# Up products by Strassen's seven block products in the feed-forward part of a decoder layer

## The chip, the cores and the metric

The kernel runs on one core of a Trainium2 chip. The metric is the device time of one execution in microseconds. In the profile PE is TensorE (its weight loads are PEld), DVE is VectorE, ACT is ScalarE, POOL is GpSimd, and SP is the engine whose queue issues most loads. The kernel is written with a layer that places semaphores and chooses the order of instructions on each engine when it is built; the order on the chip is then fixed.

## The reference, cut to what matters

The reference is one layer of a decoder: attention, an RWKV time mixing, a gated output projection, and a feed-forward part with a short convolution. It serves 2048 tokens of a prompt and 8 groups of 8 sample tokens, 2112 columns in all. The change lies in the second half:

```
x += (sigmoid(gA) * (A @ w_pa) + sigmoid(gB) * (B @ w_pb)) @ w_o
h = rmsnorm(x) * norm2_g
ug, uv = split(h @ w_up)                 # w_up: 1024 x (2 * 2816)
c = conv_b + sum_j conv_w[j] * ug shifted by 2 - j
x += (gelu(c) * uv) @ w_down
y = rmsnorm(x) * final_g
```

All values are float32. A product is made in three passes: each operand is split into a high part of fewer bits and the rest (hi and lo), and hi x hi, hi x lo and lo x hi are added.

## The kernel before

Everything is stored transposed: 128 features are the partitions of a tile, tokens are its columns. Phase 1 makes the projections, the attention and the time mixing, and leaves the gates and the outputs in DRAM. Phase 2 (`group2`) walks three groups of 704 columns, each in two chunks of 352. In a group:

1. For each of 8 output tiles the products with w_pa and w_pb (one weight tile, `w_ab`), multiplied with the gates, added on POOL and split into hi and lo (`mix`).
2. For each of 8 tiles the product with w_o over both chunks, added to x (`x2`), scaled with norm2_g and split (`h2`), squared and summed over the tiles in `rs`.
3. The second norm's factor is computed from `rs` by small matmuls and some ten short VectorE operations (`rstd_steps`). It isn't applied to `h2`: it multiplies the results. The products of the up tiles can start before it is known; line 1395 applies it to the gate half, and POOL at line 1417 applies it for the value half.
4. 22 gate tiles (`up`) and 22 value tiles (`gate`) in parts of 4, 6, 6 and 6. A tile is a product over 8 blocks of 128 features, three passes and two chunks: 48 matmuls. `up` goes on with the convolution (two taps at line 1405), the GELU by tanh, and `gate` multiplies and splits the result.
5. After each part the product with w_down for 8 tiles, added to `x2`. After the last part the final norm, which runs beside the next group's first products.

Weights come through `weights`: one load of 512 KB on SP's queue into one of two raw buffers, then in two halves a cast on ScalarE to hi (line 354, two buffers) and a subtraction to lo (line 392, three buffers). The subtraction alternates between VectorE and POOL:

```
eng = self.nc.gpsimd if self.wn % self.pool_every == 0 and not self.nopool else self.nc.vector
```

All matmuls are issued at line 287. While `self.ordered` is set, as it is from phase 1 to the end, they keep the order in which the program writes them; all else is put in order by the layer's own planner. Products go to eight PSUM buffers (`acc`).

## Time and profile before

| | us |
|---|---|
| median of 3 runs | 3466.67 (3464.66 to 3475.59) |
| the profiled execution | 3464.11 |
| its span, first to last instruction | 3462.3 |
| TensorE busy | 3288.2 |
| VectorE busy | 2165.3 |
| POOL busy | 1356.5 |
| ScalarE busy | 1313.2 |

Phase 2 begins at some 1529 us and takes the rest of the span. "Busy" is the time in which at least one instruction of the engine was at work. Two matmuls overlap in the records, so the mean duration of one is about twice the distance between two; the distance is read from the starts.

### The profile page before, as it was taken

Reading aid. Unit: us, or ns where it says so; the run is one execution under the profiler, and the core shown is the slowest. Engines: PE = TensorE matmul, PEld = TensorE weight load, DVE = VectorE, ACT = ScalarE, POOL = GpSimd, SP = SyncE. Lnnn points to the kernel's source line nnn. Section 1 sums busy time; section 2 is a strip of 40 time slices with the busy share of each in tenths; the row PEclk is TensorE's granted clock in tenths of the full one; section 3 lists DMA queues with packets and bytes.
Section 4 is the critical chain, followed back from the end, with each engine's and each line's share of the span. In section 5 each row is a group of like instructions: output and inputs, shape, how many; then the busy total and the mean of one; then the engine's idle time right before and its main releaser. Section 6 shows DMA issues by size and latency. Waiting matters only on the chain.

```text
span 3462.3 us, 59729 instructions
## 1 busy us (share of the span) xinstructions
PE 3288.2 (95%) x23574; PEld 3128.4 (90%) x23574; DVE 2165.3 (63%) x3813; ACT 1313.2 (38%) x2658; POOL 1356.5 (39%) x1375
## 2 busy tenths in 40 slices
PE   6889899899899899989999999999999999999998
PEld 6778788788788788879999999999999999999998
DVE  6767758867868858754554545555554654564554
ACT  4444434544545544423332323232232423332332
POOL 4435434435435435233333333533333442343342
PEclk9999989999999999999999999999999999999999
DMA  4442523433433433343122223612222352222222
GB/s 133 153 140 91 154 87 95 136 104 92 142 105 92 141 106 92 116 174 110 58 77 68 66 75 99 203 62 74 62 74 67 93 178 81 68 65 77 61 74 73
DMA packets 165968, 347.51 MB, mean 100 GB/s; under 512 B 59263, under 2 KB 91655, under 8 KB 165687
## 3 DMA queue, kind: packets, MB, share of 16 engines
q1 hardware_dynamic: 138263, 283.60, 26.8%
q0 software_dynamic: 8704, 37.78, 3.3%
q10 hardware_dynamic: 18720, 22.31, 1.8%
q8 instruction: 185, 3.03, 0.4%
q14 instruction: 96, 0.79, 0.1%
HBM read 302.06 MB, written 41.56 MB: 99 GB/s over the span
## 4 chain that ended last, share of the span: by engine, by line
PE 59%; DVE 3%; issue 1%; ACT 1%; DMA 0%; POOL 0%; DVEq 0%; ACTq 0%; POOLq 0%
PE acc L287 57%; PE ps L287 1%; DVE wlo L392 0%; DMA th<-outs 0%; PE psA L287 0%; DVE TX L1000 0%; PE psY L287 0%; ACT whi L354 0%; DVE LN L1002 0%; DVE x L1324 0%; PE ps L290 0%; ACT at L746 0%; DVE XV L1133 0%; DVE t_kk L930 0%; DVE G L972 0%
## 5 line engine op out<-in xcount | busy, mean ns | idle before, releaser
L392 POOL TENSOR_TENSOR wlo<-w,whi 128x512 fp32r<-128x512 f32 (+2 forms) x488 | 700.5, 1436 | 1237.0 <-ACT whi L354 987.8
L287 PE MATMUL acc<-A,whi 128*128 128x352 f32 x4992 | 1007.9, 323 | 2.3 <-DVE A L1288 1.5
L354 ACT CAST whi<-w 128x512 fp32r<-128x512 f32 (+2 forms) x984 | 537.3, 591 | 1228.1 <-PE acc L287 727.1
L287 PE MATMUL acc<-h,whi 128*128 128x384 f32 (+2 forms) x3456 | 914.5, 344 | 19.7 <-ACT raw L664 12.1
L287 PEld LDWEIGHTS acc<-A,whi 128*128 128x128 f32 x4992 | 836.0, 188 | 4.3 <-DVE A L1288 2.5
L287 PEld LDWEIGHTS acc<-h,whi 128*128 128x128 f32 x3456 | 631.6, 197 | 52.5 <-ACT raw L664 16.3
L287 PE MATMUL acc<-h,wlo 128*128 128x384 f32 (+2 forms) x1728 | 588.6, 341 | 22.0 <-DVE wlo L392 21.9
L287 PE MATMUL acc<-A,wlo 128*128 128x352 f32 x2496 | 604.5, 323 | 0.0
L287 PE MATMUL acc<-B,whi 128*128 128x352 f32 x2880 | 582.1, 323 | 0.5 <-DVE B L1291 0.4
L392 DVE TENSOR_TENSOR wlo<-w,whi 128x512 fp32r<-128x512 f32 (+2 forms) x496 | 437.4, 883 | 128.6 <-ACT whi L354 127.2
L287 PEld LDWEIGHTS acc<-B,whi 128*128 128x128 f32 x2880 | 482.3, 188 | 1.1 <-DVE B L1291 1.1
L287 PEld LDWEIGHTS acc<-A,wlo 128*128 128x128 f32 x2496 | 434.3, 188 | 0.1
L287 PEld LDWEIGHTS acc<-h,wlo 128*128 128x128 f32 x1728 | 340.5, 197 | 40.1 <-DVE wlo L392 26.9
L287 PE MATMUL acc<-B,wlo 128*128 128x352 f32 x1440 | 350.2, 323 | 0.0
L1446 DVE TENSOR_TENSOR x<-x,acc 128x352 f32<-128x352 f32 x188 | 89.5, 518 | 304.5 <-PE acc L287 304.5
L287 PEld LDWEIGHTS acc<-B,wlo 128*128 128x128 f32 x1440 | 250.9, 188 | 0.0
L1417 POOL TENSOR_TENSOR ss<-ss,ssq 128x704 f32<-128x704 f32 x66 | 113.0, 1713 | 288.6 <-DVE ss L1416 268.4
L1405 DVE SCALAR_TENSOR_TENSOR cc<-ub,vt,cc 128x704 f32<-128x704 f32 (+1 forms) x132 | 159.4, 1208 | 27.3 <-ACT cc L1399 25.8
L1395 DVE TENSOR_TENSOR ub<-acc,ssq 128x352 f32<-128x352 f32 (+1 forms) x132 | 61.6, 508 | 180.4 <-PE acc L287 179.1
L1413 ACT ACTIVATE ss<-cc 128x704 f32<-128x704 f32 x66 | 52.3, 792 | 174.9 <-DVE cc L1405 116.7
L1291 DVE SCALAR_TENSOR_TENSOR B<-ss,B 128x704 fp32r<-128x704 f32 x66 | 113.5, 1720 | 3.7 <-ACT B L1290 3.7
L1414 DVE SCALAR_TENSOR_TENSOR ss<-ss,cc 128x704 f32<-128x704 f32 x66 | 58.9, 892 | 59.6 <-ACT ss L1413 59.6
(302 smaller groups left out, 3694.5 us busy)
## 6 DMA issues: line engine op xcount, KB each, us to landing
w<-w_in SPq DMA_DIRECT2D x216, 512.0 KB, 3.6
w<-w_ug SPq DMA_DIRECT2D x66, 512.0 KB, 3.5
w<-w_uv SPq DMA_DIRECT2D x66, 512.0 KB, 3.5
w<-w_down SPq DMA_DIRECT2D x72, 384.0 KB, 3.1
th<-gates POOLq DMA_DIRECT2D x48, 352.0 KB, 4.2
gates<-raw ACTq DMA_DIRECT2D x64, 192.0 KB, 2.0
w<-w_ab SPq DMA_DIRECT2D x24, 512.0 KB, 3.9
w<-w_o SPq DMA_DIRECT2D x24, 512.0 KB, 3.5
```

Source lines behind the costliest of these rows:

```text
L287: self.pe(self.nc.tensor.matmul(out, lhsT, rhs, start=start, stop=stop), max(n * (1 if rhs.dtype == F32R else 4) / 2.4, 25))
L354: nc.scalar.copy(out=hi[:, a:b], in_=w[:, a:b])
L392: i = eng.tensor_tensor(**kw)
L1291: nc.vector.scalar_tensor_tensor(out=lo[:, :T], in0=src[:, :T], scalar=scale, in1=hi[:, :T].bitcast(F32), op0=MUL, op1=SUB)
L1395: nc.vector.tensor_tensor(out=ub[:, 2 + a:2 + e], in0=pp[:, :e - a], in1=rs[:, a:e], op=MUL)
L1405: nc.vector.scalar_tensor_tensor(out=cc[:, :n], in0=ub[:, j:j + n], scalar=self.v(wn, f), in1=cc[:, :n], op0=MUL, op1=ADD)
L1413: nc.scalar.activation(out=s[:, :T], in_=cc[:, :T], func=AF.Square, scale=GELU_A)
L1414: nc.vector.scalar_tensor_tensor(out=s[:, :T], in0=s[:, :T], scalar=1.0, in1=cc[:, :T], op0=ADD, op1=MUL)
L1417: nc.gpsimd.tensor_tensor(out=s[:, :T], in0=s[:, :T], in1=rs[:, :T], op=MUL)
L1446: nc.vector.tensor_tensor(out=x2[m][:, a:b], in0=x2[m][:, a:b], in1=pp[:, :b - a], op=ADD)
```

## The change

Two up tiles that lie side by side (features f and f+1), the two halves of their 8 feature blocks, and the two chunks of columns make a 2 x 2 by 2 x 2 product of blocks. The kernel before makes its eight block products. The change makes seven, after Strassen in Winograd's form, and adds them up on VectorE (`product`, `put`). Each block product has 4 feature blocks, three passes and one chunk: 12 matmuls of 352 columns. Four of the seven take a sum of blocks of x (`t1` to `t4`), four a sum of weight blocks (`s1` to `s4`), and the others take the blocks as they are. With sums of both chunks the second norm's factor must be on the operands, so x is multiplied with it before the products: the first chunk while the second one's w_o products run, the second after the last w_o product, in three stages. For this w_o is now walked chunk by chunk. In the first part of a group the first two products of three runs, which need the first chunk alone, are placed ahead of the others, with the order of matmuls fixed there.

The sums of weights are made once, in group 0, by POOL, and written to DRAM (`weight_sums`); later block loads read them there. Two block products share one load buffer, so a weight buffer holds 24 matmuls' worth. All subtractions of weight splits go to VectorE in phase 2 (`nopool`). The factor of one half moves from the splits to the additions after w_o and w_down.

```diff
-            self.bufs = dict(A=16, B=16, x2=8, th=4, tm=2, ub=2, cc=2, ss=2, ssq=1, carry=2, nrm=3)
+            self.bufs = dict(A=56, B=12, x2=8, th=4, ub=2, cc=2, ss=4, u=3, u3=1, ug=1, ssq=1, carry=2, nrm=3)
...
+            self.ordered = False
+            self.sums_d = [[self.dram.tile([128, 4, 4, 128], F32, name=f"sums{x}{i}") for i in range(cfg.ff // 2)] for x in "gv"]
...
+    def gemm2(self, hi, lo, xs, cs=(0, 1), wk0=0):
+
+        outs = [self.pt("acc") for _ in cs]
+        n, w = len(xs), self.cfg.tmax2 // 2
+        for k in range(n):
+            ops = [xs[k](c) for c in cs]
+            for i in range(3):
+                for o, (xh, xl) in zip(outs, ops):
+                    self.mm(o[:, :w], (hi, hi, lo)[i][:, wk0 + k, :], (xh, xl, xh)[i], k == 0 and i == 0, k == n - 1 and i == 2)
...
+    def weight_sums(self, x, i):
...
+        ap = self.A["w_ug" if x == 0 else "w_uv"]
+        v = [self.t("th", [128, self.cfg.tmax2])[:, :512] for _ in range(4)]
+        a11, a12, a21, a22 = v
+        for j, o in enumerate(v):
+            src = ap[2 * i + j // 2][:, j % 2 * 4:j % 2 * 4 + 4]
+            nc.sync.dma_start(out=o.rearrange("p (k n) -> p k n", k=4), in_=src)
+        for j, (o, p, q, op) in enumerate(((a22, a21, a22, ADD), (a21, a11, a21, SUB), (a11, a22, a11, SUB), (a12, a12, a11, SUB))):
+            nc.gpsimd.tensor_tensor(out=o, in0=p, in1=q, op=op)
+            nc.gpsimd.dma_start(out=self.sums_d[x][i][:, (0, 2, 1, 3)[j]], in_=o.rearrange("p (k n) -> p k n", k=4))
...
+    def block_weights(self, srcs):
...
+        for j, src in enumerate(srcs):
+            nc.sync.dma_start(out=w[:, j * 4:j * 4 + 4], in_=self.block_src(*src))
+        for j in range(len(srcs)):
+            a, b = j * 4, j * 4 + 4
+            nc.scalar.copy(out=hi[:, a:b], in_=w[:, a:b])
+            self.wsub(out=lo[:, a:b], in0=w[:, a:b], in1=hi[:, a:b].bitcast(F32), op=SUB)
+        return hi, lo
...
+    def block_product(self, wt, k0, xs):
+        (hi, lo), w, o = wt, self.cfg.tmax2 // 2, self.pt("acc")[:, :self.cfg.tmax2 // 2]
+        for k in range(4):
+            xh, xl = xs[k]
+            for i in range(3):
+                self.mm(o, (hi, hi, lo)[i][:, k0 + k, :], (xh, xl, xh)[i], k == 0 and i == 0, k == 3 and i == 2)
...
+    PRODUCTS = {1: ("b11", "a11"), 2: ("b21", "a12"), 3: ("b22", "s4"), 4: ("t4", "a22"), 5: ("t1", "s1"), 6: ("t2", "s2"), 7: ("t3", "s3")}
...
+        o = self.block_product(wt, k0, R.ops[self.PRODUCTS[p][0]])
...
+        def five():
+            R.put(1, 1, R.u3, R.p5)
+            nc.vector.tensor_tensor(out=R.u, in0=R.p5, in1=R.u, op=ADD)
+        if p == 1:
+            R.u = self.t("u", [128, w])
+            nc.scalar.copy(out=R.u, in_=o)
+        elif p == 2:
+            R.put(0, 0, R.u, o)
+        elif p == 6:
+            nc.vector.tensor_tensor(out=R.u, in0=o, in1=R.u, op=ADD)
+        elif p == 7:
+            R.u3 = self.t("u3", [128, w])
+            nc.vector.tensor_tensor(out=R.u3, in0=o, in1=R.u, op=ADD)
+            if R.p5 is not None:
+                five()
+        elif p == 5:
+            R.p5 = o
+            if R.u3 is not None:
+                five()
+        elif p == 4:
+            R.put(1, 0, R.u3, o)
+        else:
+            R.put(0, 1, R.u, o)
...
+    def run_products(self, seq):
+
+        for j in range(0, len(seq), 2):
+            two = seq[j:j + 2]
+            wt = self.block_weights([(R.x, R.i, self.PRODUCTS[p][1]) for R, p in two])
+            for k, (R, p) in enumerate(two):
+                self.product(R, p, wt, k * 4)
...
-            self.nopool = False
-            pa = self.gemm(hi, lo, outs[:4], 0, chunks, "acc")
-            pb = self.gemm(hi, lo, outs[4:], 0, chunks, "acc", wk0=4)
+            self.nopool = True
...
+        todo_sums = [(x, i) for i in range(cfg.ff // 2) for x in range(2)] if g == 0 else []
...
-        for m in range(8):
-            hi, lo = self.weights(A["w_o"][m])
-            ps = self.gemm(hi, lo, mix, 0, chunks, "acc")
...
-            for (a, b), pp in zip(chunks, ps):
-                nc.vector.tensor_tensor(out=x[:, a:b], in0=x[:, a:b], in1=pp[:, :b - a], op=ADD)
-            h2.append(self.split(x, "A", T, self.v("n2", m)))
...
-            x2.append(x)
-        norm = self.spawn(self.later(L_SSQ, self.rstd_steps(rs, T, "acc")))
...
+        def norm(c):
+            (a, b), more = chunks[c], [lastsq]
+            yield from self.rstd_steps(rs[:, a:b], b - a, "acc", more)
...
+        def scaled(dst, m, c, eng):
+            a, b = chunks[c]
+            if eng is nc.gpsimd:
+                eng.tensor_tensor(out=dst, in0=x2[m][:, a:b], in1=rs[:, a:b], op=MUL)
+                nc.scalar.mul(out=dst, in_=dst, mul=self.v("n2", m))
+            else:
+                eng.scalar_tensor_tensor(out=dst, in0=x2[m][:, a:b], scalar=self.v("n2", m), in1=rs[:, a:b], op0=MUL, op1=MUL)
...
+        def first_chunk():
+            for j in range(4):
+                h = self.t("ss", [128, TM])
+                h1.append(h)
+                for i, n in ((0, "b11"), (1, "b21")):
+                    d = h[:, i * w:i * w + w]
+                    scaled(d, i * 4 + j, 0, nc.vector)
+                    ops[n][j] = self.split_half(d, pool=i == 1)
...
+        for c, (a, b) in enumerate(chunks):
+            for m in range(8):
+                hi, lo = self.weights(A["w_o"][m])
+                if c == 1 and m == 7:
+                    self.ordered, self.last_pe = True, None
+                pp, = self.gemm2(hi, lo, mix, (c,))
...
+                nc.vector.scalar_tensor_tensor(out=x[:, a:b], in0=pp[:, :w], scalar=0.5, in1=x[:, a:b], op0=MUL, op1=ADD)
+                if m < 7:
+                    self.sumsq(rs, x, m, a, b)
+                else:
+                    lastsq = self.t("cc", [128, TM])[:, a:b]
+                    nc.scalar.activation(out=lastsq, in_=x[:, a:b], func=AF.Square)
+                if c == 1 and m == 1:
+                    for _ in norm(0):
+                        pass
+                    first_chunk()
+                if m % 4 == 3:
+                    sums(1)
...
-            nc.gpsimd.tensor_tensor(out=s[:, :T], in0=s[:, :T], in1=rs[:, :T], op=MUL)
...
-        def gate(f, s):
-            hi, lo = self.weights(A["w_uv"][f])
-            ps = self.gemm(hi, lo, h2, 0, chunks, "acc")
-            for (a, b), pp in zip(chunks, ps):
-                nc.vector.tensor_tensor(out=s[:, a:b], in0=s[:, a:b], in1=pp[:, :b - a], op=MUL)
-            return self.split(s, "B", T, 0.5)
...
+            def put(row, c, s, ps):
+                if ub[row] is None:
...
+                nc.vector.tensor_tensor(out=u[:, 2 + a:2 + e], in0=ps[:, :e - a], in1=s[:, :e - a], op=ADD)
...
+                done[row] += 1
+                if done[row] == 2:
+                    out[row] = conv(f + row, u)
...
+            def put(row, c, s, ps):
+                a, b = chunks[c]
+                x = ss[row][:, a:b]
+                t = self.t("ug", [128, w])
+                nc.vector.tensor_tensor(out=t, in0=ps, in1=s, op=ADD)
+                nc.vector.tensor_tensor(out=x, in0=x, in1=t, op=MUL)
+                done[row] += 1
+                if done[row] == 2:
+                    out[row] = self.split(ss[row], "B", T)
+                    if None not in out:
+                        acts.extend(lambda c, h=h: [z[:, c * w:c * w + w] for z in h] for h in out)
+            return Run(1, f // 2, put)
...
+        def second_chunk(stage):
+            for j in range(4):
+                if stage == 0:
+                    h2[j] = self.t("th", [128, TM])
+                p, q, r, s = h1[j][:, :w], h1[j][:, w:T], h2[j][:, :w], h2[j][:, w:T]
+                if stage == 0:
+                    scaled(r, j, 1, nc.vector)
+                    nc.vector.tensor_tensor(out=p, in0=r, in1=p, op=SUB)
+                    ops["t1"][j] = self.split_half(p)
+                    scaled(s, 4 + j, 1, nc.gpsimd)
+                elif stage == 1:
+                    nc.vector.tensor_tensor(out=p, in0=s, in1=p, op=SUB)
+                    ops["t2"][j] = self.split_half(p)
+                    nc.gpsimd.tensor_tensor(out=r, in0=s, in1=r, op=SUB)
+                    ops["t3"][j] = self.split_half(r, pool=True)
+                else:
+                    nc.vector.tensor_tensor(out=q, in0=q, in1=p, op=SUB)
+                    ops["t4"][j] = self.split_half(q)
+                    ops["b22"][j] = self.split_half(s, pool=True)
...
+        REST = (6, 7, 5, 4, 3)
...
+            acts = []
...
+            runs = [ups[0][0]]
+            for i, r in enumerate(gates):
+                runs += [u for u, _ in ups[i + 1:i + 2]] + [r]
+            if part is parts[0]:
+
+                fill = runs[:3]
+                for i, r in enumerate(fill):
+                    r.hold = i > 0
+                    self.run_products([(r, 1), (r, 2)])
+                    if i < 2:
+                        next(norm1, None)
+                        if i:
+                            second_chunk(0)
+                second_chunk(1)
+                second_chunk(2)
+                self.run_products([(runs[0], p) for p in (5, 6, 7, 4, 3)])
+                self.ordered = False
+                for r in runs[1:]:
+                    sums(1)
+                    if r in fill:
+                        r.hold = False
+                        for z in r.held:
+                            r.put(*z)
+                    self.run_products([(r, p) for p in ((1, 2) if r not in fill else ()) + REST])
...
+                seq = []
+                for r in runs:
+                    seq += [(r, p) for p in (1, 2) + REST]
+                for i in range(0, len(seq), 2):
+                    if i % 6 == 0:
+                        sums(1)
+                    self.run_products(seq[i:i + 2])
...
                 for (a, b), pp in zip(chunks, ps):
-                    nc.vector.tensor_tensor(out=x2[m][:, a:b], in0=x2[m][:, a:b], in1=pp[:, :b - a], op=ADD)
+                    nc.vector.scalar_tensor_tensor(out=x2[m][:, a:b], in0=pp[:, :b - a], scalar=0.5, in1=x2[m][:, a:b], op0=MUL, op1=ADD)
...
+                if m % 3 == 0:
+                    sums(1)
```

`gemm2` is `gemm` for operands that are given by chunk; a `Run` is one pair of tiles and keeps its two intermediate sums; results of the two runs that go ahead are held until their turn.

## Rows read from the trace of the kernel before

**Rows 1.** The page: busy tenths of each engine in 40 equal slices of the span.
```profile
PE   6889899899899899989999999999999999999998
...
DVE  6767758867868858754554545555554654564554
...
PEclk9999989999999999999999999999999999999999
```

**Rows 2.** Waits of TensorE from 1540 us on: total us, times, longest.
```profile
PE acc L287 <- DVE nrm L405: 5.4, 1, 5.4
```

**Rows 3.** Busy time per engine (and its instructions), clock, DMA share, GB/s, by stretch.
```profile
1530.00:1560.00 30.00, 30.00 (x186) 29.50 (x186) 15.27 (x26) 8.52 (x13) 20.85 (x27) 1.00 0.77 279
...
2020.00:2066.00 46.00, 46.00 (x286) 46.00 (x285) 26.74 (x33) 15.95 (x23) 19.45 (x16) 1.00 0.23 69
```

**Rows 4.** Timeline of VectorE, w_o products: start us, us, operation.
```profile
2244.56 0.95 DVE L1367 TENSOR_TENSOR x<-x,acc 128x352 f32<-128x352 f32 x2 [4.22 <-PE acc L287]
...
2275.28 0.95 DVE L1367 TENSOR_TENSOR x<-x,acc 128x352 f32<-128x352 f32 x2 [3.42 <-PE acc L287]
```

**Rows 5.** Timeline of TensorE, last w_down tiles, one chunk at a time.
```profile
3437.20 0.48 PE L287 MATMUL acc<-B,whi 128*128 128x352 f32 x2
3437.52 0.32 PE L287 MATMUL acc<-B,wlo 128*128 128x352 f32 x1
3437.68 0.48 PE L287 MATMUL acc<-B,whi 128*128 128x352 f32 x2
```

**Rows 6.** Groups by shape from 1500 us on: busy us, mean ns, idle before.
```profile
L287 PE MATMUL acc<-A,whi 128*128 128x352 f32 x4992 | 1007.9, 323 | 2.3 <-DVE A L1288 1.5 <-ACT A L1287 0.8
...
L287 PE MATMUL acc<-A,wlo 128*128 128x352 f32 x2496 | 604.5, 323 | 0.0
```

**Rows 7.** Timeline of POOL, up products: start us, us, operation.
```profile
2048.92 1.72 POOL L1417 TENSOR_TENSOR ss<-ss,ssq 128x704 f32<-128x704 f32 x1 [3.54 <-DVE ss L1416]
2050.59 1.74 POOL L392 TENSOR_TENSOR wlo<-w,whi 128x512 fp32r<-128x512 f32 x1
```

**Rows 8.** Timeline of VectorE, the same stretch.
```profile
2046.19 0.89 DVE L1414 SCALAR_TENSOR_TENSOR ss<-ss,cc 128x704 f32<-128x704 f32 x1 [0.86 <-ACT ss L1413]
...
2048.75 0.94 DVE L1424 TENSOR_TENSOR ss<-ss,acc 128x352 f32<-128x352 f32 x2
2049.62 1.57 DVE L392 TENSOR_TENSOR wlo<-w,whi 128x512 fp32r<-128x512 f32 x1
2051.11 1.97 DVE L1291 SCALAR_TENSOR_TENSOR B<-ss,B 128x704 fp32r<-128x704 f32 x1
...
2056.44 0.68 DVE L392 TENSOR_TENSOR wlo<-w,whi 128x512 fp32r<-128x512 f32 x1
2057.65 2.36 DVE L1405 SCALAR_TENSOR_TENSOR cc<-ub,vt,cc 128x704 f32<-128x704 f32 x2 [0.53 <-ACT cc L1399]
```

**Rows 9.** Timeline of VectorE, splits of 704 columns at a part's end.
```profile
2113.07 0.88 DVE L1291 SCALAR_TENSOR_TENSOR B<-ss,B 128x704 fp32r<-128x704 f32 x1
...
2113.87 2.48 DVE L1288 TENSOR_TENSOR A<-th,A 128x704 fp32r<-128x704 f32 x3
```

**Rows 10.** Timeline of ScalarE, the same stretch.
```profile
2045.37 0.79 ACT L1413 ACTIVATE ss<-cc 128x704 f32<-128x704 f32 x1 [3.26 <-DVE cc L1405]
...
2055.45 1.14 ACT L354 CAST whi<-w 128x512 fp32r<-128x512 f32 x2 [4.87 <-PE acc L287]
2056.56 0.98 ACT L1399 ACTIVATE cc<-ub,vt 128x704 f32<-128x704 f32 x1
```

**Rows 11.** Timeline of the final normalization: VectorE, ScalarE, POOL.
```profile
3441.61 0.16 DVE L400 TENSOR_SCALAR nrm<-nrm 128x3 int32<-128x3 int32 x1
...
3445.00 0.43 ACT L433 COPY ssq<-acc 128x352 f32<-128x352 f32 x1
...
3445.51 1.81 POOL L1321 TENSOR_TENSOR x<-x,ssq 128x352 f32<-128x352 f32 x2 [12.70 <-ACT ssq L433]
```

**Rows 12.** DMA issues of the weights: count, KB each, median us to landing.
```profile
w<-w_ug SPq DMA_DIRECT2D x66, 512.0 KB, 3.5
```

138 lines of the change are left out of this document (93 added, 45 removed).

## Prediction

> **What bounds the kernel now.** I read the page's slices first: the reader is to see that from about the eighteenth slice on TensorE is at 9 tenths in every slice with the full clock granted, while VectorE is at 4 to 6 tenths [rows 1]. That is phase 2, the only part that the change touches. Then the waits of TensorE alone in that phase: the longest is one of 5.4 us, behind the last normalization, in 1922 us [rows 2]. Then the stages: in a stretch of the up products TensorE is busy 46.00 of 46.00 us, VectorE 26.74, ScalarE 15.95, at clock 1.00 [rows 3]. So phase 2 is a queue of matmuls with nothing between them. Removing one is worth its pitch, until another engine becomes the limit. The pitch: four w_o tiles of 48 matmuls take 2275.28 - 2244.56 = 30.72 us, 160 ns each [rows 4]. Where one weight block meets only one chunk of columns, as in the Strassen products, three matmuls take 0.48 us, again 160 ns [rows 5]; the new order of matmuls has no price of its own.
>
> **What is removed.** Per pair of up tiles the kernel does 2 x 48 = 96 matmuls, that is eight block products of 12; the change does seven, 84. There are 11 gate and 11 value pairs in each of three groups: 66 x 12 = 792 matmuls go, of the 11808 in phase 2; the trace has the up products and w_ab together as 4992 + 2496 [rows 6], which is 3 x (44 + 8) x 48. The matmul count of w_o and of w_down stays. Saved: 792 x 0.160 = 126.7 us. Also gone is POOL's share of the weight splits and its product with the norm's factor (1.74 and 1.72 us each [rows 7]); as TensorE waits for neither, that gives nothing by itself.
>
> **What is added in the up products, the main cost.** I count a gate pair and a value pair together (33 of them): TensorE 168 x 0.160 = 26.9 us, before 30.7. VectorE then does:
> 14 half weight splits (before 8, of which half on POOL), 0.68 us alone [rows 8]: 9.5. 14 sums that read PSUM, two in 0.94: 6.6. Four products of 352 columns from SBUF, estimated at 0.52 from the same row: 2.1. Two convolutions, each 2.36 for the two taps beside POOL's copy, and 2 x 0.89: 8.3. Two splits of the result at 0.88 [rows 9]: 1.8. Sum 28.3 us. In a row operations overlap a little: three splits take 2.48 us, 0.80 each instead of 0.88 [rows 9]; with 0.08 less on those 34 operations where it is not already in the row the sum is 25.6. So VectorE, at 58% of this stage now, comes to between 95% and 105% of TensorE's time. ScalarE has 14 casts at 0.57, two copies out of PSUM at 0.43 and the rest as before, 0.98 once and 0.79 three times for each of two rows [rows 10, 11]: 15.5 us, no limit. The lower end is TensorE's own 26.9 per pair, the upper end VectorE with a tenth of its time lost to waits, 28.3 / 0.9 = 31.4. I take 28.3, the isolated durations: two engines that are both full don't overlap perfectly. 33 x (28.3 - 26.9) = 46 us given back (0 to 149).
>
> The Trainium skill bears on the two sums: "VectorE: DVE Perf Modes", section "The DRAIN you can't avoid", says that after each Vector operation the next one doesn't start until the pipe has emptied. By that the isolated durations hold; by the rows of three splits 0.08 us of each is shared, and the first price of the pair would be 25.6 instead of 28.3, 89 us apart over 33 pairs.
>
> What the split's move to VectorE costs is itself seen in the rows. Beside a POOL operation a VectorE split takes 1.57 instead of 0.68, and a scaled split 1.97 instead of 0.88; the sums that read PSUM are not slowed, two in 0.94 with POOL at work [rows 7, 8]. Half of 14 splits left on POOL would take up to 7 x 0.89 from VectorE, against 7 x 0.68 for doing them there. So all on VectorE is the cheaper way, and POOL is all but quiet in groups 1 and 2.
>
> **Weight sums (group 0 only).** 22 sets of four sums on POOL, 88 x some 1.7 us [rows 7], with 88 loads on SP's queue and 88 stores on POOL's. They stand ahead of weight loads on SP's queue and wait there for a th buffer, but each set is made at least two runs before it is used, and reading them back is in place of a weight block. 48 of the 88 fall in the up products; each holds up VectorE by up to 0.89, 43 us, and the rest falls where VectorE has room. I take half, as half of VectorE's time there reads PSUM or waits: 20 us (0 to 78 for all 88). The traffic per pair is 14 x 256 KB in 26.9 us, 137 GB/s; the start of phase 2 moves 279 GB/s [rows 3], so that is hidden.
>
> The Trainium skill, "SBUF — State Buffer", section "SBUF: two separate sides", calls the shared port an exclusive lock for the whole instruction. By that each of the 48 could hold VectorE for 1.7 us, 82 us, and the sum would be 62 us worse; by the rows it is 0.89, and half of it counts.
>
> **The norm on the operands.** Before, the factor was applied after the product, so nothing waited for it. Now the seven operand sums of the second chunk need it. By the order written, after the last w_o product come a fill step of 24 matmuls (3.84 us), the norm's sums over features (some 2, an estimate), a second fill step beside the reciprocal root, which with its broadcast takes 3441.61 to 3445.43, 3.8 us [rows 11], and the last of the broadcast (1.0): the factor is there some 10.7 us after. Behind it stand VectorE's 28 operations of 352 columns, 14 us, and POOL's 16 at 0.9 (two in 1.81 [rows 11]), also 14 us, and they disturb each other. So the fifth product can end some 27 us after the last w_o product. TensorE has three fills (11.5), the norm's matmuls (2.6, an estimate) and five products (9.6): 23.7. I take 5 us a group, 15 in all (0 for full cover, 36 if the operands are 12 late each time). The first chunk's operands are made under six w_o tiles, 23 us, and hidden.
>
> **w_o by chunks.** Its weights are loaded and split twice: 24 matmuls per block, 3.84 us. A raw buffer is in use for 3.5 (landing [rows 12]) + 0.33 issue + 1.14 casts + 0.68, 5.6 us, and there are two: 2.8 per block. VectorE has 2 x 0.68, 0.5 and 0.5 per block. Hidden, at 0; if each of the 48 blocks slipped 0.5, 24 us.
>
> **Sum.** -126.7 + 46 + 20 + 15 = -46 on the profiled execution's 3464.1, which is 2.6 under the median of 3466.7: 3418, and I say 3420. Its own range is 3395 to 3455.
>
> **Rivals.**
> *VectorE's queue starves TensorE (slower).* Place: two raw weight buffers and two of the high part. A block now lasts 3.84 us instead of 7.68, and of 7.68 us for two the loop takes 5.6, so a weight split may stand only 2.0 us in VectorE's queue. One pass of convolution taps takes 2.36, and puts stand there that wait for TensorE. Then VectorE too idles: at 92% use a pair takes 30.8, 33 x 3.9 = 129 given back, with 20 and 15: 3501. It is slower than before once a pair takes over 26.9 + (126.7 - 35) / 33 = 29.7 us. For it: VectorE's demand of 95 to 105%. Against it: now, with waits of its own in the convolution chain, it never delays TensorE.
> *TensorE stays the limit.* If the 25.6 holds and queues are filled well, only 10 for the sums and 10 for the norm come back: 3357. For it: the overlap of operations, and POOL's silence; against it: 95% is much to ask of an in-order queue.
> *The norm's barrier is long.* 25 us a group, if the operand sums of both chunks stand behind weight splits: 75 in place of 15, 3478, no gain at all. Against it: the fills.
> *It doesn't do what it says.* If single-chunk matmuls cost more than 160 ns the count would save less; the rows of the tail speak against it [rows 5].
>
> **Chances.** The forecast's mechanism 0.45, TensorE as limit 0.17, something in between that ends within 0.3% (10 us, about what can be told from no change here) 0.10, starvation 0.22, the barrier 0.06. So faster 0.62, same 0.10, slower 0.28. Range 3360 to 3510: under it the better part of the second rival's lower half, over it a pair of more than about 31 us.
>
> **What would show it.** Right: 792 fewer matmuls at 160 ns pitch; VectorE at 9 tenths or more in the up stages; a pair in 28 to 29 us, more in group 0; TensorE's waits there on wlo, by VectorE; one gap of some 5 us per group at the first Strassen run. Wrong: a pair under 27.3 (second rival), or over 29.7 with VectorE below 95% and waits for DMA or casts (first), or gaps over 20 us at the norm (third).

## The result: 3637.6 us, slower, and the profile after

The changed kernel takes 3637.64 us (median of 4 runs, 3633.36 to 3646.39) against 3465.66 for the kernel before on the same chip: a ratio of 1.0499, 95% interval 1.0473 to 1.0525. The forecast was 3420, so even the sign was wrong.

The head of the page and three of its 40-slice lines, to be held against [rows 1]:

```profile
span 3644.6 us, 60526 instructions
PE 3279.5 (90%) x22818; PEld 3055.2 (84%) x22818; DVE 2595.8 (71%) x4844; ACT 1496.8 (41%) x3096; POOL 1055.6 (29%) x1270
PE   7888899899899999897777999988999998899998
DVE  6757668768768778667666757667865856876765
PEclk9998899999999999998889999999999999899999
```

There are 756 matmuls fewer: 792 less, as forecast, and 36 more for norms that are now made by chunks. But TensorE's row of nines has holes: a long one in slices 19 to 22 (group 0), and one at each later group's start (slices 27 and 28, 34 and 35); beside the first and the last the granted clock is lower too.

Where the time is, by stage. A stage ends with the last VectorE or ScalarE operation that reads its products; "lost" is its length less its matmuls at 0.160 us; as those are counted by where they start, a loss is good to about a microsecond. Group 1 stands for groups 1 and 2, which agree within 4 us in each of these stages. All in us:

| stage | before, group 1 | lost | after, group 0 | lost | after, group 1 | lost |
|---|---|---|---|---|---|---|
| w_ab | 64.6 | 3.1 | 59.9 | 1.9 | 61.4 | 0.6 |
| w_o | 61.4 | 0.0 | 90.6 | 29.3 | 85.2 | 23.4 |
| first part (2 pairs), up | 65.2 | 3.6 | 102.2 | 47.4 | 85.2 | 31.4 |
| its down | 31.0 | 0.4 | 44.9 | 12.9 | 31.2 | 0.3 |
| next part (3 pairs), up | 93.2 | 0.9 | 136.0 | 55.3 | 86.3 | 5.5 |
| its down | 46.5 | 0.6 | 55.5 | 11.5 | 46.4 | 0.5 |
| another part, up | 93.2 | 0.9 | 86.2 | 5.7 | 86.3 | 5.8 |

A part of three pairs does gain, 93.2 to 86.3, once nothing else disturbs it. Everything in phase 2 together lost 30 us before and 334 after; the difference of 304 eats the 126.7 of the matmuls and 178 more.

The longest waits on SP's queue in group 0 (us in total, times, longest):

```profile
SPq L1348 <- DMA sumsg<-th: 116.2, 41, 8.4
SPq L1348 <- DMA sumsv<-th: 96.3, 30, 8.3
SPq L344 <- DVE wlo L392: 83.4, 19, 18.4
```

Line 1348 loads the blocks for the weight sums. It stands in the queue with the weight loads, and for 212 us it waits until the stores of the set before have landed and given their buffers back. The waits of TensorE in group 1, from 2350 to 2521 (w_o and the first part), where the whole phase had one wait of 5.4 us and one of 0.4 before [rows 2]:

```profile
PE acc L287 <- DVE A L1303: 8.9, 8, 2.3
PE acc L287 <- DVE nrm L420: 8.7, 2, 5.1
PE acc L287 <- DVE wlo L392: 7.6, 4, 3.4
```

And the engines at the first Strassen run of group 1 (columns: stretch and its length, then PE, PEld, DVE, ACT and POOL busy, PEclk, DMA share, GB/s):

```profile
2445.00:2455.00 10.00, 5.18 (x28) 4.12 (x26) 10.00 (x11) 5.47 (x12) 8.05 (x7) 0.95 0.09 35
2455.00:2465.00 10.00, 6.26 (x16) 4.37 (x17) 10.00 (x16) 4.40 (x10) 5.28 (x5) 0.50 0.00 0
2465.00:2475.00 10.00, 8.09 (x29) 7.05 (x29) 8.05 (x13) 3.32 (x8) 5.27 (x8) 0.67 0.56 178
```

VectorE is busy 10.00 of 10.00 us twice, TensorE little over half, and after the gaps TensorE's granted clock is 0.50, the 1.2 GHz level: 16 matmuls keep it busy for 6.26 us there.

### The profile page after: what moved, and what is told of

Its sections match the earlier page's. It is cut to its first block, busy times and chain, and to the rows that moved or that the text cites. A ratio compares the mean times of both kernels' runs of the same rounds, so it can differ in the third digit from the quotient of the medians.

```text
span 3644.6 us, 60526 instructions
## 1 busy us (share of the span) xinstructions
PE 3279.5 (90%) x22818; PEld 3055.2 (84%) x22818; DVE 2595.8 (71%) x4844; ACT 1496.8 (41%) x3096; POOL 1055.6 (29%) x1270
## 5 line engine op out<-in xcount | busy, mean ns | idle before, releaser
L287 PE MATMUL acc<-A,whi 128*128 128x352 f32 x4656 | 1132.1, 333 | 68.1 <-ACT whi L1370 35.8
L392 DVE TENSOR_TENSOR wlo<-w,whi 128x512 fp32r<-128x512 f32 (+2 forms) x1017 | 752.4, 761 | 246.1 <-ACT whi L354 183.1
L287 PE MATMUL acc<-A,wlo 128*128 128x352 f32 x2328 | 739.3, 334 | 60.1 <-DVE wlo L392 58.2
L354 ACT CAST whi<-w 128x512 fp32r<-128x512 f32 (+2 forms) x768 | 414.3, 583 | 820.7 <-PE acc L287 559.7
L287 PE MATMUL acc<-h,wlo 128*128 128x384 f32 (+2 forms) x1728 | 589.5, 341 | 23.8 <-DVE wlo L392 23.7
L1370 ACT CAST whi<-w 128x512 fp32r<-128x512 f32 x462 | 270.3, 618 | 457.3 <-PE acc L287 229.0
L392 POOL TENSOR_TENSOR wlo<-w,whi 128x512 fp32r<-128x512 f32 x213 | 298.6, 1403 | 388.7 <-ACT whi L354 260.8
L1684 DVE SCALAR_TENSOR_TENSOR x<-acc,x 128x352 f32<-128x352 f32 x188 | 89.7, 519 | 265.8 <-PE acc L287 265.8
L1350 POOL TENSOR_TENSOR th<-th 128x512 f32<-128x512 f32 x88 | 116.5, 1324 | 152.2 <-DMA th<-w_uv 81.2
L1565 DVE SCALAR_TENSOR_TENSOR cc<-ub,vt,cc 128x704 f32<-128x704 f32 (+1 forms) x132 | 130.6, 999 | 10.2 <-ACT cc L1559 9.2
L1588 DVE TENSOR_TENSOR ub<-acc,u 128x352 f32<-128x352 f32 (+1 forms) x132 | 67.2, 509 | 51.7 <-PE acc L287 49.0
L1468 POOL TENSOR_TENSOR th<-th 128x704 f32<-128x704 f32 x24 | 49.0, 2040 | 168.1 <-DVE th L1467 168.1
```

The costliest lines, as they stand in the source:

```text
L287: self.pe(self.nc.tensor.matmul(out, lhsT, rhs, start=start, stop=stop), max(n * (1 if rhs.dtype == F32R else 4) / 2.4, 25))
L354: nc.scalar.copy(out=hi[:, a:b], in_=w[:, a:b])
L392: i = eng.tensor_tensor(**kw)
L1350: nc.gpsimd.tensor_tensor(out=o, in0=p, in1=q, op=op)
L1370: nc.scalar.copy(out=hi[:, a:b], in_=w[:, a:b])
L1468: nc.gpsimd.tensor_tensor(out=ta[:, :T], in0=ta[:, :T], in1=tb[:, :T], op=ADD)
```

## The experiments

All were timed in turns with the kernel before, which had medians of 3457 to 3463 us beside them and 3466 beside the changed kernel. Times without a ratio are medians, to be held against the changed kernel's 3638; a step of under some 10 us between two of them is within that drift, and the stages of the profiles, not the medians, say what it is.

### The weight sums

**e2_no_sums.** `todo_sums` is empty and the sum blocks are read from the plain weights.

> The changed kernel with the weight sums left out: none is computed or stored, and the block loads that would read a sum read a plain block of the same size. Products, splits and additions are as many. Theory A: group 0 (755 us) comes to what groups 1 and 2 need, less the late final norm that group 0 does not have, some 650: 3530 to 3545. Theory C, with POOL's sums holding up VectorE as priced before the result (20 to 43 us): 3595 to 3620.

This takes 3520.7 us, ratio 1.0163 (1.0135 to 1.0192): 117 us come back, 112 of them in group 0 by the two profiles. It is the largest piece, and still not enough.

**e1_sums_pool** moves the loads to POOL's queue; **f1_loads_alone** also moves the convolution's two-column copies off POOL:

```
-            nc.sync.dma_start(out=o.rearrange(...), in_=src)
+            nc.gpsimd.dma_start(out=o.rearrange(...), in_=src)
...
-            nc.gpsimd.tensor_copy(out=ub[:, 0:2], in_=self.prevc[:, f, :])
+            nc.scalar.copy(out=ub[:, 0:2], in_=self.prevc[:, f, :])
```

> The changed kernel with one edit: the 88 loads for the weight sums are issued on POOL's queue instead of SP's; the same bytes move. Theory A (those loads wait on SP's queue for the stores of the set before, and weight loads stand behind them; TensorE starves in group 0): 60 to 90 us of the 3638 go, 3550 to 3580, and in group 0 most of TensorE's waits on casts and lo halves go with them; some may come back because POOL's small copies for the convolution now stand behind those loads. Theory B (the memory traffic of the sums is too much): no change, 3638. Theory C (VectorE's own load in the up products is the loss): no change.

> The changed kernel with the loads for the weight sums on POOL's queue, as in the run before, and the two small copies of the convolution (two columns each) on ScalarE instead of POOL, so that in the up products nothing of the convolution stands behind those loads. Theory A, mended (in the run before the same wait moved from SP's queue to POOL's, where VectorE's taps waited 40 us for the copies): now 60 to 100 us of 3638 go, 3540 to 3580. Theory B (traffic of the sums, or their own round trips, set the time): 3620 or more.

The times are 3644.1 us (no gain) and 3621.5 us (16 less). On POOL's queue the same wait stood ahead of those small copies, for which the convolution on VectorE then waited 40.3 us; with the copies gone from there the first part of three pairs in group 0 still took 118.2 us, against 136.0 in the changed kernel. The theory that it is SP's queue alone fell. What holds up that part instead is seen after the next run.

**h2_no_arith** keeps all loads and stores and drops POOL's additions (`nc.gpsimd.tensor_tensor(out=o, in0=p, in1=q, op=op)` in `weight_sums`).

> The changed kernel, without the arithmetic of the weight sums: the four blocks are loaded and stored as they are, on the same queues and buffers; leaves out the sums. Theory (the waits of loads and stores at the head of SP's queue cost the 117 us): 30 to 60 us faster at most, as a set's round trip gets only the 4 x 1.3 us of POOL shorter, 3575 to 3610. Rival (POOL's 88 operations beside VectorE cost it): back to the kernel without sums, 3520 to 3540.

This takes 3608.4 us, as the theory has it: without the 88 additions 29 us come back (21 by the ratios to the kernel before, 1.0499 and 1.0437). SP's waits on the stores remain:

```profile
SPq L1348 <- DMA sumsg<-th: 84.1, 39, 5.6
SPq L1348 <- DMA sumsv<-th: 60.9, 33, 5.4
```

But the 29 us are not all that the additions cost. The first part of three pairs in group 0, in the changed kernel, h2_no_arith, f1_loads_alone and e2_no_sums (columns as above):

```profile
1828.60:1964.60 136.00, 99.16 (x506) 90.37 (x506) 101.95 (x124) 44.53 (x71) 66.03 (x79) 0.86 0.63 209
```

```profile
1825.50:1943.50 118.00, 94.96 (x504) 89.69 (x503) 73.76 (x125) 44.63 (x72) 18.42 (x40) 0.90 0.65 213
```

```profile
1813.90:1932.10 118.20, 97.93 (x523) 92.01 (x521) 101.92 (x123) 44.30 (x82) 63.69 (x79) 0.88 0.63 201
```

```profile
1782.00:1867.80 85.80, 82.96 (x504) 80.27 (x503) 73.41 (x124) 42.96 (x71) 5.05 (x12) 1.00 0.39 124
```

The same operations keep VectorE busy for 101.95 us beside 33 additions on POOL and for 73.41 without them: 0.86 us for each addition. Without the additions VectorE is as free as without sums, and the part still takes 118 us, with TensorE waiting 19.9 us for casts, which ScalarE makes and for which it waits on the weight loads. With the loads off SP's queue VectorE is the busy one, and the part takes 118 us too, with TensorE waiting longest for low halves of weights. So there are two costs, VectorE's slower work beside POOL and the late weights, and each hides most of the other: taking away either brings 18 of this part's 50 us. The 117 us can't be shared out between them by taking 29 off.

**i2_after_pinned** holds every load of the sums behind the weight load that precedes it in the program, with an order-only dependency.

> The changed kernel with each load of the sums held behind the weight load that stands before it in the program, so that no set runs ahead of its place. All of the computation kept. Theory (the distance decides: Strassen's runs need a set per 14.4 us, less than a set's 17 to 18 us, so that a later place only moves the wait): under 35 us faster, 3600 to 3640. Rival (the sets stood too early, and the place decides): 70 to 110 faster, 3530 to 3570.

This takes 3621.6 us, 16 less (10 by the ratios): the place alone does not do it. The Strassen runs need a set per 14.4 us (two a pair of 28.8), and in the changed kernel one comes round in 16.5 us (18 sets from 1714.8 to 1995.7 us). That this difference is what remains was not tested by itself.

### The norms

**e3_early_final** drains the last group's final norm after the second w_ab tile instead of the eighth; **f2_norm_steps** hands on the generator step by step, with a weight tile or two between the sums and the broadcast, for the final norm and for the first chunk's (here the lines of the first chunk's):

```
-                if c == 1 and m == 1:
-                    for _ in norm(0):
-                        pass
+                if c == 1 and m == 0:
+                    norm0 = norm(0)
+                    next(norm0)
+                if c == 1 and m == 2:
+                    next(norm0, None)
                     first_chunk()
```

> The changed kernel with the final norm of the group before written after the second of the eight w_ab tiles instead of after the eighth (in the kernel before it ran in between, by polling from gemm, which gemm2 does not do). Theory: in groups 1 and 2 the w_o products wait for that norm's steps (5 us), for the x2 buffers that it still holds (3 to 4 us) and run at the lower clock after it; 12 to 18 us a group go, 3602 to 3614. Rival: the x2 buffers are late anyway because the stores of the output are: under 5 us.

> The changed kernel with the two norms that are written in one go (the final norm of the group before, and the first chunk's) written in two steps with one or two tiles of products between the sums over features and the broadcast. Theory: five times TensorE's in-order queue stands 4 to 8 us at a broadcast that waits for VectorE's root, and runs on at the lower clock for some us; 7 to 11 us each, 35 to 55 in all, 3583 to 3603. The first run of that kind, which only moved the whole norm earlier, moved the loss with it (9 us less). Rival (the loss in w_o is its weight loads, with 24 matmuls per block): under 15 us.

The times are 3629.3 and 3612.4 us. In the first the 5.0 us wait at the broadcast only moved (to 2302.42, among the w_ab products). In the second w_o of groups 1 and 2 lost 6.6 us instead of 23.4 and 21.9, and w_ab 3 more: that is the 25 us.

**e4_bar_dve** makes the second chunk's operands on VectorE alone, **f5_six_fills** puts six runs ahead of the barrier instead of three.

> The changed kernel with POOL's 16 operations of the second chunk's operands put on VectorE. In the trace VectorE's 28 operations there take 1.25 us beside POOL and 0.51 alone. Theory A (the two engines hold each other up): 44 operations at 0.45 are 20 us instead of some 26, 4 to 8 us a group, 3614 to 3626. Rival (POOL's share is a real help): VectorE's chain is 16 x 0.5 = 8 us longer, 3650 to 3660.

> The changed kernel with parts of 6, 6, 6 and 4 tiles instead of 4, 6, 6 and 6, and the first two products of all six runs of the first part placed ahead of the second chunk's operands (before: three runs). TensorE then has 23 us of matmuls to do instead of 11.5 while the norm and the operands are made. Theory (the loss of 30 us per group there is missing cover, and the lower clock that follows): 12 to 18 us a group come back, 3585 to 3600. Rival (VectorE's work is only put off, and the held results come in a burst after it): under 15 in all, 3623 or more.

The times are 3630.5 and 3648.0 us. VectorE's operations by line in the 40 us around the barrier (columns: line, engine, form, count, then busy us, mean ns), first the changed kernel from 2440, then e4 from 2430:

```profile
L1303 DVE TENSOR_TENSOR A<-ss,A 128x352 fp32r<-128x352 f32 x12 | 10.7, 895 | 0.1
L1500 DVE SCALAR_TENSOR_TENSOR th<-x,vt,ssq 128x352 f32<-128x352 f32 x4 | 4.3, 1090 | 0.0
L1588 DVE TENSOR_TENSOR ub<-acc,u 128x352 f32<-128x352 f32 x3 | 1.6, 520 | 1.3 <-PE acc L287 1.3
```

```profile
L1303 DVE TENSOR_TENSOR A<-ss,A 128x352 fp32r<-128x352 f32 x12 | 6.2, 516 | 0.1
L1500 DVE SCALAR_TENSOR_TENSOR th<-x,vt,ssq 128x352 f32<-128x352 f32 x8 | 4.3, 576 | 0.0
```

Beside POOL an operation with both inputs in SBUF takes 895 ns on the average instead of 516 (half of these twelve some 510, the others 1130 to 1570); one that reads PSUM keeps its 520. Without POOL each is short, but VectorE has all of them: the first parts of groups 1 and 2 still lose 27 to 30 us. With six fills they lose 29.5 us, now in a part of three pairs. Group 1 as a whole is 9 us shorter with them and group 2 as long as before; the median is higher because group 0, with the sums, loses more. So a lack of cover is at most a small piece of the loss.

**g2_no_factor** runs on **g1_mended** (below) and takes away the wait for the factor alone:

```
-                eng.scalar_tensor_tensor(out=dst, in0=x2[m][:, a:b], ..., in1=rs[:, a:b], op0=MUL, op1=MUL)
+                eng.scalar_tensor_tensor(out=dst, in0=x2[m][:, a:b], ..., in1=x2[m][:, a:b], op0=MUL, op1=MUL)
```

> The kernel with the three places mended, and the operands of the up products multiplied by x instead of by the norm's factor: leaves out the norm on the operands, with the same number and size of operations, so that no operand waits for the factor. Theory (the 30 us lost at the first up part are VectorE's own work: 44 operations of 352 columns at 0.52 = 23 us for the second chunk's operands, in a stage where it has no room): gains under 8 us a group, at most 20 in all, and the first up parts still lose 20 to 30. Rival (the wait for the factor, sums, root and broadcast, some 10 us, is what TensorE pays for, with the lower clock behind it): the first up parts lose under 12, 50 to 60 us less in all.

This takes 3589.3 us against 3632.7, 43 less, between the two. The first parts lose 16 to 17 us instead of 27 to 28, and w_o 2.8 instead of 6.7. So of the 28 us some 11 are the wait for the factor, with what it brings on the clock. Of the rest nearly 4 are what two pairs lose in any part; the other 12 to 13 I put down to VectorE's work on the operands. That is argued, not shown: of the 9.4 us that TensorE still waits there in group 1, 5.0 are for low halves of weights, which VectorE makes.

### Where the split is made, and VectorE's load

**f4_pool_splits** sets `nopool` to False, so that half of the weight splits go back to POOL.

> The changed kernel with every second weight split on POOL again, as in the kernel before. By the rows of before, a split on POOL holds VectorE up by up to 0.89 us where doing it there costs 0.68: 3660 to 3690. Rival, if VectorE is what limits the up products and POOL's time is free: a part of three pairs goes from 86 us towards 81, 27 us or more less, 3600 to 3615.

This takes 3696.2 us, 59 more. In sum the prediction's claim that all splits on VectorE is the cheaper way holds, but not everywhere: by the profiles 29 us of the loss lie in group 0 and 19 in group 2, while group 1 is 1 us longer.

**g1_mended** is the control of the next run: sums made in phase 1, norms in steps, operands on VectorE. **g3_light_vector** adds one ScalarE function in place of two ScalarE and two VectorE operations a row; **g4_before_light** makes the same edit in the kernel before:

```
-            nc.scalar.activation(out=s[:, :T], in_=cc[:, :T], func=AF.Square, scale=GELU_A)
-            nc.vector.scalar_tensor_tensor(out=s[:, :T], in0=s[:, :T], scalar=1.0, in1=cc[:, :T], op0=ADD, op1=MUL)
-            nc.scalar.activation(out=s[:, :T], in_=s[:, :T], func=AF.Tanh, scale=GELU_B)
-            nc.vector.scalar_tensor_tensor(out=s[:, :T], in0=s[:, :T], scalar=1.0, in1=cc[:, :T], op0=ADD, op1=MUL)
+            nc.scalar.activation(out=s[:, :T], in_=cc[:, :T], func=AF.Gelu_apprx_tanh)
```

> All of the computation kept, three places mended at once: the 88 weight sums are made in phase 1 (halves of 256 columns, loads at one w_in tile, sums and stores two tiles later, own buffers), the final norm and the first chunk's norm are written in steps with weight tiles between sums, root and broadcast, and the second chunk's operands are made on VectorE alone. Theory (the loss is additive: sums 117, norm steps 25, POOL beside VectorE 7): 3638 - 117 - 25 - 7 = 3489, plus what 176 POOL operations beside a TensorE that is busy 9 tenths of phase 1 cost there, 0 to 40: 3480 to 3525. Group 0 then lasts about as long as groups 1 and 2, some 645, and the first part of the up products still loses some 28 us in each group. Rival (the waits hide one another, so mending all gives more than the sum): under 3470. Rival (phase 1 pays as much as phase 2 did): over 3560, phase 1 over 1580 us.

> The kernel with the three places mended, and the gate's nonlinearity by one ScalarE function (tanh approximation) in place of two ScalarE and two VectorE operations a row: all of the computation kept. VectorE gets 4 x 0.89 = 3.6 us a pair less. Theory (the up products are limited by VectorE's queue, 28.8 us a pair against TensorE's 26.9): parts of three pairs fall from 86.3 to 81 - 82.5, 33 pairs give 45 to 62 us; with some 4 us less in each first part, 3420 to 3450 if the mended kernel has 3489. Rival (the pair's time is set by the two raw weight buffers and their chain of load, cast and split, not by VectorE's load): parts stay at 85 or more, under 15 us gained.

> The kernel before, with the same one ScalarE function for the gate's nonlinearity: all of the computation kept. Control for the light-vector run: in the kernel before TensorE is the limit in the up products (busy 46.00 of 46.00) and VectorE at 58%, so both theories expect no change: within 5 us of the kernel before.

g1_mended takes 3632.7 us (ratio 1.0500): phase 2 fell by 153 us to 1960, but phase 1 ended at 1676 instead of 1531 us. The rival was right that phase 1 pays. g3_light_vector takes 3556.2 us, 76 less; g4_before_light has a ratio of 1.0001 (0.9987 to 1.0016). One part of three pairs in the light kernel, and the same stage of the changed one (columns as above):

```profile
2532.00:2612.50 80.50, 80.50 (x504) 80.50 (x503) 64.68 (x112) 38.78 (x64) 4.82 (x12) 1.00 0.44 133
```

```profile
2551.70:2637.90 86.20, 83.28 (x506) 80.48 (x506) 73.44 (x124) 42.74 (x70) 5.80 (x12) 1.00 0.39 123
```

With VectorE at 64.68 of 80.50, TensorE is busy all the time and a pair takes 26.8 us; at 73.44 of 86.20 it takes 28.7, though VectorE is idle for 15% of it. The rival of the raw buffers falls with that. The edit also takes two ScalarE operations and the waits between the two engines out of each row's chain, so VectorE's load and the length of the chain are not told apart. The same edit gives the kernel before nothing: there TensorE had no wait to lose.

### Where the sums belong

**h1_pinned** is g3 with loads and additions of the sums held at their places in phase 1. **h3_mixed_light** keeps plain products in group 0, where it makes the sums, and in the first part of each group, beside which the second chunk's operands are made; **h4_mixed** is the same without the ScalarE function.

> The light-vector kernel (3556), with the sums still in phase 1, but each load held behind the weight load and each sum behind the POOL split that stand before it in the program, so that the sums spread over phase 1 instead of running ahead as fast as buffers allow (in that kernel they were over at 718 us). All of the computation kept. Theory (phase 1's extra 145 us is time at the heads of the SP and POOL queues, which a set as early as possible spends waiting for its buffers and transfers): phase 1 ends near 1550 to 1600 and the whole takes 3440 to 3490. Rival (it is the sums' work itself, POOL's arithmetic slowing VectorE and the added traffic, wherever it stands): phase 1 still ends near 1650 to 1680, 3530 to 3560.

> Plain products where Strassen's were late: the whole first group, in which the weight sums are then made, and the first part (two pairs) of each later group, beside which the second chunk's operands are made; Strassen's products in the nine-pair rest of groups 2 and 3. Norms in steps, second-chunk operands on VectorE, and the gate's nonlinearity by one ScalarE function. All of the computation kept. Theory: 2 x 9 pairs x 3.84 = 69 us of matmuls saved, parts of three pairs at 80.6; the first group as before plus 0 to 20 for the sums, w_o some 6 later in each group: 3462 - 69 + 20 + 10 = 3410 to 3435. Rival (the sums hold up plain products as they did Strassen's): the first group over 700 us, 3480 or more.

> The same without the one ScalarE function: VectorE keeps its two operations a row. Parts of three pairs go back to 86 to 88, that is 6 x 6 to 7 us: 3445 to 3475, the same as the kernel before; all of the computation kept. Rival (with operands ready and no sums, VectorE keeps up): within 10 us of the light one.

h1_pinned takes 3534.9 us (21 less; phase 1 still ends at 1652: the rival was right, and where in phase 1 the cost arises stays open). h3_mixed_light takes 3527.3 and h4_mixed 3593.4 us. In h4 groups 1 and 2 take 637 and 643 us, no less than before (641 and 638): in group 1 the three parts of three pairs gain 21 us together, and w_o, the first part and the products with w_down give 16 of it back; group 2 loses 5. Without the relief of VectorE nothing is left even there. The first parts of groups 1 and 2, with the operands beside plain products, lose 6.9 and 7.5 us in h4 and under 4 in h3, against 27 to 28 beside Strassen's products in g1_mended: there the operands, and the wait for the factor, have room. In h3 groups 1 and 2 take 611 us each, 26 to 30 less than before, but group 0 takes 750 instead of 636: even plain products, with twice the time per weight load, are held up. TensorE's longest wait from 1529 to 2300 us, SP's waits on the stores, and SP's queue at one set show why (columns of the last three lines: start, length, queue, line, operation, count):

```profile
PE acc L287 <- ACT whi L354: 67.5, 17, 10.5
SPq L1348 <- DMA sumsv<-th: 118.1, 36, 9.2
SPq L1348 <- DMA sumsg<-th: 109.2, 38, 9.2
```

```profile
1697.35 7.90 SPq L1348 DMA_DIRECT2D th<-w_uv  x4
1705.34 0.86 SPq L344 DMA_DIRECT2D w<-w_uv  x2
1714.27 1.19 SPq L1348 DMA_DIRECT2D th<-w_ug  x2
```

A set comes round in 17 us (1697.35 to 1714.27: loads, four additions, stores), 15.8 on the average. But from 1680 to 2003 us 84 of these loads, 21 sets, stand beside 38 weight loads: the planner had put one set to 1.8 weight loads, at most 13.9 us of matmuls, where the program has one to 2.9. The weight loads wait out the difference, and TensorE waits for their casts.

**i1_mixed_pinned** is h3 with one set per three weight tiles, each load held behind its weight load:

```
-            nc.sync.dma_start(out=o.rearrange("p (k n) -> p k n", k=4), in_=src)
+            i_ = nc.sync.dma_start(out=o.rearrange("p (k n) -> p k n", k=4), in_=src)
+            self.tc.add_manual_dep(i_.ins, self.last_w, ORDER, reason="issue order")
...
+                if (at + row) % 3 == 0 and at < 9:
+                    sums(1)
```

> The light mixed kernel (3527, first group 750 us), with one set of weight sums per three weight tiles of the first group's up and down products (17 to 23 us apart), each load held behind the weight load that it follows. All of the computation kept. Theory (SP's queue: a set takes 17 to 18 us from its first load to its last store, and the next set's loads wait for it ahead of weight loads if they come sooner): the first group falls to 645 to 670, the kernel to 3415 to 3450, faster than the kernel before. Rival (the traffic and POOL's work cost it wherever they stand): first group over 700, over 3480.

This takes 3426.7 us, ratio 0.9905 (0.9890 to 0.9921), as the theory has it: faster than both kernels, though than the kernel before by 1% only. The page's head and PE line, then SP's queue at one set and its waits in group 0:

```profile
span 3423.5 us, 60240 instructions
PE 3233.8 (94%) x23178; PEld 3064.2 (90%) x23178; DVE 2335.0 (68%) x4472; ACT 1418.8 (41%) x2995; POOL 1012.7 (30%) x1222
PE   6889899899899899989999999999999999999998
```

```profile
1802.90 5.12 SPq L344 DMA_DIRECT2D w<-w_uv  x2
1808.13 1.80 SPq L1348 DMA_DIRECT2D th<-w_uv  x4
1815.72 9.47 SPq L344 DMA_DIRECT2D w<-w_uv  x2
```

```profile
SPq L1348 <- DMA sumsg<-th: 12.7, 6, 3.5
SPq L1348 <- DMA sumsv<-th: 8.8, 3, 3.6
```

Four loads are out in 1.80 us instead of 7.90, the waits on stores fall from h3's 227 us to 22, and group 0 takes 646: the same 22 sets, beside the same plain products, on the same queue, engine and buffers, for some 10 us instead of 114. There is now one set to 3.2 weight loads. So what costs there is sets that follow one another faster than they come round. The run changed the places and the holding together, and which of the two did more was not taken apart; and with plain products no sum is needed before group 1, which in the changed kernel it is.

## Why the prediction was wrong

**The matmuls: right.** 792 fewer at 160 ns, -126.7. The light kernel does 504 matmuls of Strassen's products in 80.50 us, 160 ns each.

**The up products: the size right, the reason half.** Forecast 28.3 us a pair, measured 28.8; over the nine parts of three pairs in the kernel without sums 55.6 us are lost, near the 46 forecast for all 33 pairs. But VectorE is busy 73.44 / 3 = 24.5 us a pair, not 28.3. So that the two figures agree is in part luck. TensorE's weight loads in that part wait for low halves (`wlo`) and casts, 5.7 us in all, which is what it loses:

```profile
PEld acc L287 <- DVE wlo L392: 4.3, 6, 2.0
PEld acc L287 <- ACT whi L1370: 1.4, 4, 0.5
```

I take it that splits stand behind puts and convolutions that wait themselves: the in-order queue of the first rival, at a mild price. VectorE's records in that part, of thirteen groups that add up to 81.0:

```profile
L392 DVE TENSOR_TENSOR wlo<-w,whi 128x512 fp32r<-128x512 f32 x40 | 26.6, 684 | 2.9 <-ACT whi L1370 2.9
L1565 DVE SCALAR_TENSOR_TENSOR cc<-ub,vt,cc 128x704 f32<-128x704 f32 x12 | 11.3, 946 | 1.6 <-ACT cc L1559 1.5
L1588 DVE TENSOR_TENSOR ub<-acc,u 128x352 f32<-128x352 f32 x12 | 6.3, 522 | 4.7 <-PE acc L287 4.5 <-issue 0.2
```

The taps take 0.946 each, where I had 1.18 beside POOL's copy, and 81.0 us of durations fit into 73.44 busy. The Trainium skill, "VectorE: DVE Perf Modes", section "The DRAIN you can't avoid", has the next operation wait until the pipe is empty, and adds that one that isn't held starts earlier. The trace agrees with the second: 0.06 of each is shared, so isolated durations are too high a price for a row.

**The weight sums: the first step that failed.** "They stand ahead of weight loads on SP's queue and wait there for a th buffer, but each set is made at least two runs before it is used." That looks at when a set is needed. What counts is what stands behind the set's loads while they wait: the next weights. I gave the queue nothing and POOL's arithmetic 20 (0 to 78); together they cost 117 (e2_no_sums). Taking away the arithmetic alone brings 29 (h2_no_arith), taking the loads off SP's queue alone 16 (f1_loads_alone), as each hides the other. The arithmetic's own price was right: 0.86 us of VectorE's time for an addition where I had 0.89. Halving it for operations that read PSUM or wait was not borne out, and that the loads' waits hold up nothing was wrong. For the arithmetic the Trainium skill's exclusive lock ("SBUF — State Buffer", section "SBUF: two separate sides") would give up to 1.3 us, the length of an addition, for each of 88, 116 in all, an estimate; the profiles have 0.86 us of VectorE's time for each, and in the kernel's time 0.33 come back.

**The norm on the operands: 15 forecast, some 70 measured.** In the kernel without sums the first parts lose 92.5 us; 10.2 of that they lost before, and 12 are what six pairs lose anyway. This step failed too. I compared two delays, 27 us against 23.7 of cover, and took the difference. But the operands are 28 operations of VectorE and 16 of POOL beside it in a stage where VectorE's queue already sets the pace. The runs show that more cover does little (f5_six_fills) and that the factor's wait, with the lower clock after its gaps, is 11 of 28 a group (g2_no_factor); that most of the rest is the operands' own work is argued. In size the third rival, which I gave 0.06, was the case.

**w_o by chunks: "Hidden, at 0", with 24 as the far end; 52.5 measured** without sums. Not by weight loads, which the step priced: the new product function (`gemm2`) does not call `self.poll()`, as `gemm` does, and both norms are written in one go. (With `self.ordered` off, as it is here, the planner may also move matmuls; it did not put others in between.) So TensorE meets the broadcast right behind the sums and waits for the root, 5.05 us at 2356.10 and 3.66 at 2409.03, with a clock of 0.75 and 0.81 around. I read the norm's barrier only after w_o, and never asked what the old function did between matmuls. In steps, and with no sums beside it (g1_mended), w_o loses 20 us in all.

**The sum.** Beside the matmuls' -126.7 stand 50 for the parts of three pairs (55.6 less the 5 they lost before), 70 and 12 for the first parts, 52.5 for w_o and 117 for the sums: +175, where phase 2 has +178. The forecast had 81. The matmuls came out as forecast and the up products nearly (62 for 46); the sums, the operands and w_o, 35 in the forecast, came to 240. The range ended at 3510 because each cost was bounded by its own work, never by what waits behind it.

## What to carry to other kernels

Count a transfer that needs a buffer by how long it can stand at the head of its queue, and space such sets by their full way round (here 16 to 17 us), not by when they are needed. Two costs of one stage can hide each other: taking away one at a time shows too little of both, so take away both as well. Cutting the matmuls of a full TensorE is worth only what the next engine's in-order queue lets through: VectorE at 85% busy (73.44 us, 91% of the 80.6 that TensorE needs) already delayed TensorE, at 80% it did not. Work that is put beside a stage for cover has to fit into that stage's slowest engine. A new loop in place of an old one has to be asked for the small things that the old one did on the way.

## What was not expected of the hardware

An engine need not be full to set the pace: 73.44 of 86.20 us busy, and 1.9 us a pair late. At group 1's barrier two gaps of 1.52 and 1.73 us and the beginning of a third were followed by a granted clock of 0.50 (1.2 GHz) from 2453.95 to 2471.02 us, where from 2455 to 2465 us 16 matmuls kept TensorE busy for 6.26 us, so that the barrier cost it more than its waits. VectorE's 28 operations there took either 0.51 to 0.58 us or, beside POOL, 1.13 to 1.57, and none anything between, so that their mean describes neither. The sums' traffic and POOL's additions cost phase 1 121 us when spread (h1_pinned) and phase 2's first group some 10 (i1_mixed_pinned). In phase 1 VectorE, POOL and SP's queue already serve many short chains; whether one of them pays, and which, was not taken apart.
